# Reading two activations back from DRAM by quarters of columns and turning them on VectorE, in the gate, output-projection and routing stage of a decoder layer

## The chip, the cores and the metric

The kernel runs on one core of a Trainium2 chip, as one launch. The metric is the device time of the whole launch in microseconds (us). Three runs of the kernel before gave 4114.98, 4118.72 and 4122.0 us, so the median is 4118.72 us. PE is TensorE, DVE is VectorE, ACT is ScalarE, POOL is GpSimd and SP is SyncE, whose queue issues most of the DMAs.

## The reference

The layer works on x of 4096 rows and 1024 columns in float32. Two groups of heads, retention (`ret`) and a gated delta rule (`dn`), each make 512 columns. The part that this change touches comes after them:

```python
ret = rmsnorm(ret).reshape(B, T, RET_WIDTH) * jax.nn.silu(r_g.astype(jnp.float32))
...
dn = rmsnorm(dn, dn_norm_w[l]).reshape(B, T, DN_WIDTH) * jax.nn.silu(d_z.astype(jnp.float32))
mix = jnp.concatenate([ret, dn], axis=-1).astype(x.dtype) @ w_out[l]
x = x + gate1[:, None, :] * mix
h2 = modulate(rmsnorm(x, norm2_w[l]), shift2, scale2)
ffn = hierarchical_moe(h2, w_group[l], b_group[l], w_expert[l], b_expert[l], ...)
```

Here `r_g` and `d_z` are columns of the input projection, so their product with `w_in` is also computed in this stage. `hierarchical_moe` first takes the logits of 4 groups and 32 experts (36 columns) of each row of `h2`, picks a group and two experts in it, and later runs the experts on the rows sorted by expert.

## The kernel before

The kernel has four stages. Stage A makes the normed and modulated input, transposed, as a pair of arrays `hh_d` and `hl_d` in DRAM (a rounded part and the remainder), and the retention. Stage B makes the delta rule. Stage C (`phase_c`, `c_tile`, `route`) is the one that changes. Stage D runs the experts.

Precise products are made of three passes of the array: `split` writes a rounded copy of an operand (`hi`, on ScalarE, L71) and the remainder (`lo`, on VectorE, L72), and `proj` (L290 to L292) adds the products `hi`·`hi`, `hi`·`lo` and `lo`·`hi` for each of 8 blocks of 128 input columns. One `proj` with 512 output columns is therefore 24 matmuls.

Stage C goes over 32 tiles of 128 rows. `c_tile` is a generator of one tile's work, cut by `yield` into steps:

1. Load the tile's columns of `hh_d` and `hl_d` and its rows of `ret_d` and `dn_d`. Two `proj` (48 matmuls `pgz`) give the gates, ScalarE applies silu (`sg`), GpSimd multiplies it into `mix`.
2. Turn `mix`: 8 float32 transposes on TensorE into PSUM (`ptm`, L939), then `split` from PSUM into `mh` and `ml`.
3. Two `proj` with `w_out` (48 matmuls `poC`), add to x on VectorE (L946), store x in `acc_d`, square on ScalarE (L950), reciprocal root (`rsqrt_b`, mostly on GpSimd), scale on VectorE (L960), add the shift on GpSimd (L961), store the result in `h2_d`.
4. Turn `h2`: 8 float32 transposes on TensorE (`pth`, L968), copied by ScalarE into `hTC`.
5. The router: 8 float32 matmuls of 36 output rows (`pl`, L979), the bias on VectorE (L980), and at a block's end (4 tiles) a transpose of the logits (`plt`).

`phase_c` calls these steps one tile ahead: the gates of tile t+1 stand before the projection of tile t, and step 5 of tile t-1 after it. `route` then works on a block of tiles, on VectorE for the most part. There are 10 blocks: seven of 4 tiles, one of 2 and two of 1.

The order on each engine is not that of the code. A scheduler works out a list of instructions for each engine, and each engine runs its list strictly in order, waiting at an instruction until its operands are there. The same holds for the DMAs that SP issues. All matmuls of the stage share PE's list, and `acc_d`, `h2_d`, the loads of `hhC`, `hlC`, `mix` and x share SP's.

Of the kernel before, what the change touches and what calls it, by code (L numbers as in the profile page):

```python
# [19 lines left out]
P = 128  # L20
# [33 lines left out]
class Kern:  # L54
# [27 lines left out]
    def wblock(self, src, eng, n=512, extra=None, scale=None, pool=None):  # L82
# [3 lines left out]
        for k2 in range(KD // 2):  # L86
            rows = slice(2 * k2 * P, (2 * k2 + 2) * P)
            raw = two(self.wtile("wraw", F32))
            eng.dma_start(raw[:, :, 0:512], src[rows].rearrange("(a p) n -> p a n", p=P))
# [10 lines left out]
    def setup(self):  # L100
# [8 lines left out]
        self.dn_d = dp.tile([T, 512], F32, name="dn_d")  # L109
        self.h2_d = dp.tile([T, D], F32, name="h2_d")  # L110
# [333 lines left out]
    def phase_b(self):  # L444
        tc, nc, T = self.tc, self.nc, self.T
        with tc.tile_pool(name="B", bufs=2) as p:
# [15 lines left out]
            def next_weights():  # L462
# [5 lines left out]
                self.dnw = self.xp.tile([P, 1], F32, name="dnw", bufs=1)  # L468
                nc.sync.dma_start(self.dnw, self.dn_norm_w.rearrange("o p -> p o"))
# [338 lines left out]
    def phase_c(self):  # L808
        tc, nc, T = self.tc, self.nc, self.T
        with tc.tile_pool(name="C", bufs=2) as p:  # L810
            LG, LT, run = {}, {}, []

            def tile_(t):
                run.append(self.c_tile(p, t, LG, LT))
                next(run[t])
# [6 lines left out]
            self.wo.append(self.wo_block(1, p))  # L822

            self.A2, self.B2 = A2, B2 = [p.tile([P, D], F32, name=n, bufs=1) for n in ("A2", "B2")]
            n2 = p.tile([P, D], F32, name="n2", tag="h2", bufs=2)
# [11 lines left out]
            self.br, self.wr = br, wr  # L837
# [28 lines left out]
            for t in range(NT + 1):  # L866
                if t + 1 < NT:
                    tile_(t + 1)
                if t < NT:
                    next(run[t])  # L870
                if t >= 1:
                    next(run[t - 1])
# [3 lines left out]
                if t < NT:  # L876
                    next(run[t])
# [10 lines left out]
    def wo_block(self, i, pool=None):  # L888
# [5 lines left out]
        def scale(raw, k2):  # L894
            g = g1[:, None].to_broadcast([P, 2, 512])
            if k2 < 2:
                nc.vector.tensor_tensor(raw, raw, g, op=ALU.mult)
            else:
                nc.vector.scalar_tensor_tensor(raw, raw, self.dnw, g, op0=ALU.mult, op1=ALU.mult)

        return self.wblock(self.w_out[0][:, 512 * i:512 * i + 512], nc.scalar, scale=scale, pool=pool)

    def c_tile(self, p, t, LG, LT):
        nc = self.nc
        rows = slice(t * P, (t + 1) * P)
        hs = []
# [680 lines left out]
```

## Time and profile before

| | |
|---|---|
| median of three runs | 4118.72 us |
| the profiled execution's own time | 4121.5 us |
| its span, first to last instruction | 4119.7 us |
| busy over the span: PE, DVE, ACT, POOL | 95%, 60%, 39%, 37% |
| mean DMA rate | 140 GB/s |
| mean granted TensorE clock | 0.981 of full speed |
| stage C, first to last projection | about 1807 to 2625 us |

The profile is one execution of the program. The lines of its views name the line of the code (L939), the engine, the tiles that are written and read, and times. Matmuls overlap in the array, so the time that one occupies PE is read from the distance between starts, or from the chain of waits, which gives each its share. The profiled execution's time is 2.8 us above the median of the runs.

### The profile page before, as it was taken

How to read it: one execution, taken by the hardware profiler on the slowest of the kernel's cores; microseconds unless marked ns; L12 is line 12 of the kernel's file. 1: busy time of each engine (PE TensorE's matmuls, PEld its weight loads, DVE VectorE, ACT ScalarE, POOL GpSimd, SP SyncE). 2: the span in 40 equal slices, each digit the busy share in tenths (PEclk: the TensorE clock that was granted, in tenths of full speed). 3: DMA queues.
4: the chain of work that ended last, by engine and by line, in shares of the span. 5: the costliest groups of instructions: out<-in, count | busy, mean ns of one | idle time of the engine just before them, and what ended most of it. 6: DMA issues, size and time to landing. Idle time of an engine off the chain costs nothing.

```text
span 4119.7 us, 73091 instructions
## 1 busy us (share of the span) xinstructions
PE 3911.6 (95%) x27074; PEld 3515.6 (85%) x27074; DVE 2467.8 (60%) x6437; ACT 1587.3 (39%) x3298; POOL 1525.5 (37%) x2133
## 2 busy tenths in 40 slices
PE   5999999999999999979999999699999999999997
PEld 4888889899999999968888888598888888888886
DVE  6555543577778777742222222557777777777785
ACT  3433443444544444421122211234444444444453
POOL 2333334234443344222333333433333443454442
PEclk9999999999999999989999999799999999999999
DMA  6443322422222222453333333346666675666673
GB/s 194 137 128 123 98 91 89 115 59 74 58 60 66 74 61 60 118 158 120 118 123 123 123 123 111 119 142 209 204 225 226 216 237 193 232 209 206 225 233 125
DMA packets 459759, 577.48 MB, mean 140 GB/s; under 512 B 97296, under 2 KB 361720, under 8 KB 459400
## 3 DMA queue, kind: packets, MB, share of 16 engines
q1 hardware_dynamic: 411112, 464.72, 36.4%
q0 software_dynamic: 45632, 102.64, 7.4%
q10 hardware_dynamic: 2656, 5.42, 0.4%
q8 instruction: 214, 3.51, 0.4%
q14 instruction: 145, 1.19, 0.1%
HBM read 458.94 MB, written 166.78 MB: 152 GB/s over the span
## 4 chain that ended last, share of the span: by engine, by line
PE 77%; DVE 8%; DMA 8%; issue 3%; ACT 2%; SPq 1%; POOL 1%; DVEq 0%; POOLq 0%; ACTq 0%
PE ph L1410 5%; PE ph L1411 5%; PE ph L1409 5%; PE pjB L523 4%; PE pjB L522 4%; PE pjB L524 4%; PE py L1502 3%; PE py L1503 3%; PE py L1504 3%; PE pgz L291 3%; PE pgz L292 3%; PE pgz L290 3%; PE poC L291 3%; PE poC L292 3%; PE poC L290 3%
## 5 line engine op out<-in xcount | busy, mean ns | idle before, releaser
L1410 PE MATMUL ph<-xl,whD 128*128 128x240 f32 (+7 forms) x2048 | 588.2, 288 | 3.5 <-DVE xl L72 3.2
L1409 PE MATMUL ph<-xh,whD 128*128 128x240 f32 (+7 forms) x2048 | 580.1, 289 | 11.6 <-DVE ssD L1330 6.5
L1411 PE MATMUL ph<-xh,wlD 128*128 128x240 f32 (+7 forms) x2048 | 586.4, 288 | 0.0
L71 ACT ACTIVATE whD<-rawD 128x1024 fp32r<-128x1024 f32 x384 | 400.9, 1056 | 316.0 <-PE py L1503 125.9
L72 DVE TENSOR_TENSOR wlD<-rawD,whD 128x1024 fp32r<-128x1024 f32 x384 | 460.9, 1218 | 35.1 <-ACT whD L71 33.2
L522 PE MATMUL pjB<-hhB,whi 128*128 128x260 f32 x1536 | 443.1, 291 | 9.5 <-DVE cv L530 4.2
L523 PE MATMUL pjB<-hlB,whi 128*128 128x260 f32 x1536 | 440.7, 288 | 6.3 <-DMA hlB<-hl_d 6.1
L524 PE MATMUL pjB<-hhB,wlo 128*128 128x260 f32 x1536 | 440.8, 288 | 0.0
L1409 PEld LDWEIGHTS ph<-xh,whD 128*128 128x128 f32 x2048 | 388.9, 191 | 17.6 <-DVE ssD L1330 7.1
L1410 PEld LDWEIGHTS ph<-xl,whD 128*128 128x128 f32 x2048 | 391.1, 191 | 8.2 <-DVE xl L72 5.3
L1411 PEld LDWEIGHTS ph<-xh,wlD 128*128 128x128 f32 x2048 | 390.9, 191 | 1.9
L522 PEld LDWEIGHTS pjB<-hhB,whi 128*128 128x128 f32 x1536 | 289.0, 189 | 13.9 <-DMA hhB<-hh_d 4.5
L523 PEld LDWEIGHTS pjB<-hlB,whi 128*128 128x128 f32 x1536 | 290.3, 189 | 10.7 <-DMA hlB<-hl_d 8.3
L524 PEld LDWEIGHTS pjB<-hhB,wlo 128*128 128x128 f32 x1536 | 290.1, 189 | 1.6
L532 POOL TENSOR_TENSOR cv<-cv,cv 128x256 f32<-128x256 f32 x192 | 142.0, 740 | 399.2 <-DVE Xd L602 140.5
L1502 PE MATMUL py<-whD,hh 128*128 128x512 f32 (+4 forms) x640 | 259.5, 405 | 12.4 <-DVE hh L69 7.6
L1503 PE MATMUL py<-wlD,hh 128*128 128x512 f32 (+4 forms) x640 | 252.8, 395 | 0.0
L1504 PE MATMUL py<-whD,hl 128*128 128x512 f32 (+4 forms) x640 | 245.9, 399 | 4.6 <-DVE hl L72 4.3
L946 DVE TENSOR_TENSOR xC<-poC,xC 128x512 f32<-128x512 f32 x64 | 44.2, 691 | 329.6 <-PE poC L292 329.6
L1537 POOL DMA_INDIRECT acc_d<-ag,to x80 | 112.2, 1403 | 345.9 <-DVE ag L1510 257.9
L530 DVE SCALAR_TENSOR_TENSOR cv<-pjB,cw,cv 128x256 f32<-128x256 f32 x384 | 183.1, 479 | 78.8 <-ACT cv L528 71.5
L290 PE MATMUL pj<-whi,hh 128*128 128x512 f32 x512 | 205.8, 402 | 6.0 <-ACT whi L71 6.0
(449 smaller groups left out, 10234.4 us busy)
## 6 DMA issues: line engine op xcount, KB each, us to landing
rawD<-in_w_dram SPq DMA_DIRECT2D x384, 512.0 KB
wa<-in_w_ada_dram SPq DMA_DIRECT2D x48, 512.0 KB
hhB<-hh_d SPq DMA_DIRECT2D x64, 260.0 KB
hlB<-hl_d SPq DMA_DIRECT2D x64, 260.0 KB
acc_d<-xC SPq DMA_DIRECT2D x32, 520.0 KB
wraw<-in_w_in_dram SPq DMA_DIRECT2D x32, 512.0 KB
hh_d<-hh SPq DMA_DIRECT2D x16, 1024.0 KB
hl_d<-hl SPq DMA_DIRECT2D x16, 1024.0 KB
```

The lines of the kernel that those rows point to most:

```text
L71: nc.scalar.activation(hi, src, AF.Copy)
L72: (e_lo or nc.vector).tensor_tensor(lo, src, hi.bitcast(F32) if hasattr(hi, "bitcast") else hi, op=ALU.subtract)
L290: nc.tensor.matmul(out, a, hi, start=(k == 0), stop=False)
L522: nc.tensor.matmul(pj, wh, hh[k], start=(k == 0), stop=False)
L523: nc.tensor.matmul(pj, wh, hl[k], start=False, stop=False)
L524: nc.tensor.matmul(pj, wl, hh[k], start=False, stop=(k == KD - 1))
L1409: nc.tensor.matmul(ph[nm], hi, xh[:, k, 0:n], start=(k == 0), stop=False)
L1410: nc.tensor.matmul(ph[nm], hi, xl[:, k, 0:n], start=False, stop=False)
L1411: nc.tensor.matmul(ph[nm], lo, xh[:, k, 0:n], start=False, stop=(k == KD - 1))
L1502: nc.tensor.matmul(py[i], a, hi, start=(k == 0), stop=False)
L1503: nc.tensor.matmul(py[i], a, lo, start=False, stop=False)
L1504: nc.tensor.matmul(py[i], b, hi, start=False, stop=(k == 3))
```

## The change

The transposes on TensorE go from the stage, and the router changes its form.

- The gated rows `mix` are stored to a new array `mg_d` in DRAM, and `h2` is stored to `h2_d` as before. A new function `turn` reads the 128 rows back in four DMAs (`seg`), each of 256 columns for 32 partitions, turns 32x32 blocks with two VectorE transposes of 128x512, and splits each half: ScalarE writes the rounded part, VectorE the remainder. This is done for `mix` (into `mh`, `ml`) and for `h2` (into `hT`). To match the new order of the columns, the rows of `w_out` and of the router's weights are loaded in the same order, by more and smaller DMAs.
- The router's product is made of 8 matmuls of the rounded type with 72 output rows and 256 columns in place of the 8 float32 ones, and the four parts are put together by two VectorE operations and one small float32 matmul (`plt`) per tile.
- The gates run two tiles ahead. `rsqrt_b` and the shift of `h2` are on VectorE instead of GpSimd.

```diff
+            if seg:
+                for q in range(4):
+                    r = 256 * q + 64 * k2
+                    eng.dma_start(raw[32 * q:32 * q + 32, :, 0:512], src[r:r + 64].rearrange("(a i) n -> i a n", i=32))
+            else:
+                eng.dma_start(raw[:, :, 0:512], src[rows].rearrange("(a p) n -> p a n", p=P))
...
+        self.mg_d = dp.tile([T, D], F32, name="mg_d")
...
-                self.dnw = self.xp.tile([P, 1], F32, name="dnw", bufs=1)
-                nc.sync.dma_start(self.dnw, self.dn_norm_w.rearrange("o p -> p o"))
+                self.dnw = self.xp.tile([P, KD], F32, name="dnw", bufs=1)
+                nc.vector.memset(self.dnw, 1.0)
+                for q in (2, 3):
+                    for a in range(2):
+                        nc.sync.dma_start(self.dnw[32 * q:32 * q + 32, 4 * a:4 * a + 4],
+                                          self.dn_norm_w.rearrange("o (k i) -> i (o k)", i=32))
...
+        with tc.tile_pool(name="C", bufs=2, reuse_waits="tile") as p:
...
+            tile_(1)
...
-            wr = p.tile([P, KD, 36], F32, name="wr", bufs=1)
-            nc.sync.dma_start(wr[:, :, 0:4], self.w_group[0].rearrange("(k p) n -> p k n", p=P))
-            nc.sync.dma_start(wr[:, :, 4:36], self.w_expert[0].rearrange("(k p) n -> p k n", p=P))
-            br = p.tile([36, 1], F32, name="brt", bufs=1)
+            wr = p.tile([P, KD, 36], F32, name="wr", tag="hT", bufs=1)
+            for q in range(4):
+                w = wr[32 * q:32 * q + 32]
+                for c, src in ((slice(0, 4), self.w_group), (slice(4, 36), self.w_expert)):
+                    nc.sync.dma_start(w[:, :, c], src[0][256 * q:256 * q + 256].rearrange("(k i) n -> i k n", i=32))
+            self.wr = p.tile([P, KD, 72], F32R, name="wr2", bufs=1)
+            self.split(self.wr[:, :, 0:36], self.wr[:, :, 36:72], wr)
...
+            self.sel = p.tile([72, 36], F32, name="sel", bufs=1)
+            nc.vector.tensor_tensor(self.sel, self.ident[0:72, 0:36], self.ident[0:72, 36:72], op=ALU.add)
...
-                if t + 1 < NT:
-                    tile_(t + 1)
+                if t + 2 < NT:
+                    tile_(t + 2)
                 if t < NT:
                     next(run[t])
-                if t >= 1:
-                    next(run[t - 1])
...
                 if t < NT:
+                    next(run[t])
                     next(run[t])
                 if t >= 1:
                     for _ in run[t - 1]:
...
-            g = g1[:, None].to_broadcast([P, 2, 512])
-            if k2 < 2:
-                nc.vector.tensor_tensor(raw, raw, g, op=ALU.mult)
-            else:
-                nc.vector.scalar_tensor_tensor(raw, raw, self.dnw, g, op0=ALU.mult, op1=ALU.mult)
-
-        return self.wblock(self.w_out[0][:, 512 * i:512 * i + 512], nc.scalar, scale=scale, pool=pool)
-
-    def c_tile(self, p, t, LG, LT):
+            for a in range(2):
+                k = 2 * k2 + a
+                nc.vector.scalar_tensor_tensor(raw[:, a], raw[:, a], self.dnw[:, k:k + 1], g1, op0=ALU.mult, op1=ALU.mult)
+
+        return self.wblock(self.w_out[0][:, 512 * i:512 * i + 512], nc.scalar, scale=scale, pool=pool, seg=True)
...
-        mix = []
         for i, d in enumerate((self.ret_d, self.dn_d)):
-            mix.append(self.xp.tile([P, 512], F32, name="mix", tag=f"x{i}", bufs=2))
-            nc.sync.dma_start(mix[i], d[rows, :])
-        for i in range(2):
+            mix = self.xp.tile([P, 512], F32, name="mix", tag=f"x{i}", bufs=2)
+            nc.sync.dma_start(mix, d[rows, :])
             pg = self.psum([P, 512], "pgz", "pj")
             sg = self.xp.tile([P, 512], F32, name="sg", bufs=1)
             self.proj(pg, *hs, 0, self.gz[i], 0, 512)
             nc.scalar.activation(sg, pg, AF.Silu)
-            nc.gpsimd.tensor_tensor(mix[i], mix[i], sg, op=ALU.mult)
+            nc.gpsimd.tensor_tensor(mix, mix, sg, op=ALU.mult)
+            nc.sync.dma_start(self.mg_d[rows, 512 * i:512 * i + 512], mix)
+        yield
+        mh, ml = (p.tile([P, KD, P], F32R, name=n, bufs=1) for n in ("mh", "ml"))
+        self.turn(mh, ml, self.mg_d[rows])
         xw = self.wtile("xC", F32)
         x = xw[:, 0:D]
         nc.gpsimd.memset(xw[:, D:], 0.0)
         nc.sync.dma_start(x, self.x[0, rows, :])
         yield
-
-        if t < 2:
-            mh, ml = ([self.xp.tile([P, 4, P + 2], F32R, name=n, tag="h", bufs=10)[:, :, 0:P] for _ in range(2)]
-                      for n in ("mhx", "mlx"))
-        else:
-            mh, ml = (p.tile([P, KD, P], F32R, name=n, bufs=1).rearrange("p (i k) n -> i p k n", i=2)
-                      for n in ("mh", "ml"))
-        for i in range(2):
-            pt = self.psum([P, 4, P], "ptm", "tp")
-            for a in range(4):
-                nc.tensor.transpose(pt[:, a], mix[i][:, a * P:(a + 1) * P], self.ident)
-            self.split(mh[i], ml[i], pt)
-        yield
         for i in range(2):
             po = self.psum([P, 512], "poC", "ch")
-            self.proj(po, [mh[k // 4][:, k % 4] for k in range(KD)], [ml[k // 4][:, k % 4] for k in range(KD)], 0,
-                      self.wo[i], 0, 512)
+            self.proj(po, [mh[:, k] for k in range(KD)], [ml[:, k] for k in range(KD)], 0, self.wo[i], 0, 512)
             nc.vector.tensor_tensor(x[:, 512 * i:512 * i + 512], po, x[:, 512 * i:512 * i + 512], op=ALU.add)
         nc.sync.dma_start(self.acc_d[rows, :], xw)
         ss = p.tile([P, 1], F32, name="ssC", bufs=2)
-        h2 = p.tile([P, D], F32, name="h2", bufs=2)
+        h2 = self.wtile("h2C", F32)[:, 0:D]
         nc.scalar.activation(h2, x, AF.Square, accum_out=ss)
         nc.vector.tensor_scalar(ss, ss, 1.0 / D, EPS, op0=ALU.mult, op1=ALU.add)
-        last = t == self.NT - 1
-        self.rsqrt_b(p, ss, ss, 1, None if last else nc.gpsimd)
-        if last:
-            for i in range(2):
-                c = slice(512 * i, 512 * i + 512)
-                nc.vector.scalar_tensor_tensor(h2[:, c], x[:, c], ss, self.A2[:, c], op0=ALU.mult, op1=ALU.mult)
-                nc.vector.tensor_tensor(h2[:, c], h2[:, c], self.B2[:, c], op=ALU.add)
-        else:
-            nc.vector.scalar_tensor_tensor(h2, x, ss, self.A2, op0=ALU.mult, op1=ALU.mult)
-            nc.gpsimd.tensor_tensor(h2, h2, self.B2, op=ALU.add)
+        self.rsqrt_b(p, ss, ss, 1)
+        nc.vector.scalar_tensor_tensor(h2, x, ss, self.A2, op0=ALU.mult, op1=ALU.mult)
+        nc.vector.tensor_tensor(h2, h2, self.B2, op=ALU.add)
         nc.sync.dma_start(self.h2_d[rows, :], h2)
         yield
-        hT = self.wtile("hTC", F32)[:, 0:D].rearrange("p (k n) -> p k n", k=KD)
-        for i in range(2):
-            pt = self.psum([P, 4, P], "pth", "tp")
-            for a in range(4):
-                nc.tensor.transpose(pt[:, a], h2[:, (4 * i + a) * P:(4 * i + a + 1) * P], self.ident)
-            nc.scalar.activation(hT[:, 4 * i:4 * i + 4], pt, AF.Copy)
+        hT = p.tile([P, KD, 2, P], F32R, name="hT", bufs=1)
+        self.turn(hT[:, :, 0], hT[:, :, 1], self.h2_d[rows])
         yield
         q, j = self.block_of[t]
         n = len(self.blocks[q])
         if j == 0:
             LG[q] = p.tile([P, 4, 36], F32, name="LG", bufs=1)[:, :n]
-            LT[q] = p.tile([36, 4, P], F32, name="LT", bufs=1)
-        LG, LT = LG[q], LT[q]
-        pl = self.psum([36, P], "pl", "lv")
+
+        pl = self.psum([72, 2, P], "pl", "lv")
         for k in range(KD):
             nc.tensor.matmul(pl, self.wr[:, k], hT[:, k], start=(k == 0), stop=(k == KD - 1))
-        nc.vector.tensor_scalar(LT[:, j], pl, self.br, None, op0=ALU.add)
-        if j == n - 1:
-            pt = self.psum([P, 4, 36], "plt", "tp")
-            for i in range(n):
-                nc.tensor.transpose(pt[:, i], LT[:, i], self.ident[0:36, 0:36])
-            nc.vector.tensor_copy(LG, pt[:, :n])
+        LT = p.tile([72, P], F32, name="LT", bufs=1)
+        nc.vector.tensor_scalar(LT, pl[:, 0], self.br, None, op0=ALU.add)
+        nc.vector.tensor_tensor(LT, pl[:, 1], LT, op=ALU.add)
+        pt = self.psum([P, 36], "plt", "tp")
+        nc.tensor.matmul(pt, LT, self.sel, start=True, stop=True)
+        nc.vector.tensor_copy(LG[q][:, j], pt)
+
+    def turn(self, hi, lo, src):
+
+        nc = self.nc
+        seg = self.wtile("seg", F32)[:, 0:D]
+        for q in range(4):
+            nc.sync.dma_start(seg[32 * q:32 * q + 32].rearrange("j (b c) -> j b c", b=4),
+                              src[:, 256 * q:256 * q + 256].rearrange("(b j) c -> j b c", b=4))
+        for a in range(2):
+            k = slice(4 * a, 4 * a + 4)
+            tr = self.xp.tile([P, 4, P + 2], F32, name="tr", tag="h", bufs=10)[:, :, 0:P]
+            nc.vector.transpose(tr.rearrange("p k (b j) -> p b k j", b=4),
+                                seg.rearrange("p (b k i) -> p b k i", b=4, k=KD)[:, :, k])
+            self.split(hi[:, k], lo[:, k], tr)
```

The `split` at the end of `turn` and the loop of `phase_c` give the list of PE another order at the end of a tile's projection. In these rows `poC` is the projection, `pl` the router and `pgz` the gates. Before, the router's operand `hTC_23636` comes from `h2_23515`, the tile before the one whose projection (`poC_23675`) has just ended:

```order
L290 MATMUL poC_23675<-whi_21054,mh_23620 128x512
L291 MATMUL poC_23675<-wlo_21055,mh_23620 128x512
L292 MATMUL poC_23675<-whi_21054,ml_23621 128x512
L979 MATMUL pl_23727<-hTC_23636,wr_21065 36x128 x8
L984 MATMUL plt_23737<-K_66,LT_23162 128x36 x3
L292 MATMUL pgz_23819<-whi_20673,hlC_23813 128x512
L290 MATMUL pgz_23819<-whi_20673,hhC_23809 128x512
```

With the change `hT_24547` is turned from `h2C_24526`, which is computed from the projection `poC_24498` itself:

```order
L298 MATMUL poC_24498<-wlo_21091,mh_24454 128x512
L299 MATMUL poC_24498<-whi_21090,ml_24455 128x512
L975 MATMUL plt_24573<-sel_21187,LT_24570 128x36
L970 MATMUL pl_24753<-hT_24547,wr2_21180 72x256 x4
L297 MATMUL pgz_24586<-whi_20656,hhC_24576 128x512
L298 MATMUL pgz_24586<-wlo_20657,hhC_24576 128x512
L297 MATMUL pgz_24617<-whi_20723,hhC_24576 128x512
L298 MATMUL pgz_24617<-wlo_20724,hhC_24576 128x512
L970 MATMUL pl_24753<-hT_24547,wr2_21180 72x256 x4
L299 MATMUL pgz_24586<-whi_20656,hlC_24580 128x512
```

So the router's product of a tile has moved from behind the next tile's projection to directly behind its own. Only `plt` stands between the two (at a block's end also the small matmuls of `route`), and the gates of the tile after the next stand behind it.

On SP, before, the store of `h2` is followed by loads that don't depend on it, and nothing in the stage reads `h2_d`:

```order
L917 DMA mix_23557<-ret_d_70 128x512
L917 DMA mix_23559<-dn_d_71 128x512
L962 DMA h2_d_72<-h2_23327 128x1024
L947 DMA acc_d_73<-xC_23241 128x1040
L927 DMA xC_23617<-in_x_dram 128x1024
L911 DMA hlC_24040<-hl_d_69 128x4x128
L911 DMA hlC_24042<-hl_d_69 128x4x128
L911 DMA hhC_24224<-hh_d_68 128x4x128
L911 DMA hhC_24226<-hh_d_68 128x4x128
L917 DMA mix_23815<-ret_d_70 128x512
L917 DMA mix_23817<-dn_d_71 128x512
```

With the change the store is followed at once by the four reads of the same rows, and the loads for the next gates stand behind those:

```order
L950 DMA acc_d_74<-xC_24469 128x1040
L958 DMA h2_d_73<-h2C_24526 128x1024
L983 DMA seg_24548<-h2_d_73 32x4x256 x4
L983 DMA seg_24648<-mg_d_72 32x4x256 x3
L926 DMA hhC_24576<-hh_d_68 128x4x128
L926 DMA hhC_24578<-hh_d_68 128x4x128
L926 DMA hlC_24580<-hl_d_69 128x4x128
L926 DMA hlC_24582<-hl_d_69 128x4x128
L983 DMA seg_24648<-mg_d_72 32x4x256
L944 DMA xC_24661<-in_x_dram 128x1024
L937 DMA mg_d_72<-mix_24584 128x512
L931 DMA mix_25072<-ret_d_70 128x512
```

The loads of `hhC` and `hlC` have thus moved behind a read that waits for the store of `h2`.

On VectorE, before, a tile has two additions, three small operations and the scaling between its projection and the next tile's split:

```order
L946 TENSOR_TENSOR xC_23241<-poC_23461,xC_23241 128x512
L946 TENSOR_TENSOR xC_23241<-poC_23487,xC_23241 128x512
L980 TENSOR_SCALAR LT_23162<-pl_23539,brt_21068 36x128
L951 TENSOR_SCALAR ssC_23514<-ssC_23514 128x1
L431 TENSOR_SCALAR rb_y_23518<-ssC_23514 128x1
L432 TENSOR_SCALAR rb_y_23518<-rb_y_23518 128x1
L960 SCALAR_TENSOR_TENSOR h2_23515<-xC_23241,ssC_23514,A2_21058 128x1024
L72 TENSOR_TENSOR ml_23621<-ptm_23622,mh_23620 128x512
L72 TENSOR_TENSOR ml_23621<-ptm_23629,mh_23620 128x512
L946 TENSOR_TENSOR xC_23429<-poC_23649,xC_23429 128x512
```

With the change (the list from the last round of the reciprocal root on; `seg_24548` is read from `h2_d`, `seg_24648` from `mg_d`):

```order
L442 TENSOR_TENSOR rb_t_24530<-rb_y_24529 128x1
L443 TENSOR_TENSOR rb_t_24530<-rb_t_24530,rb_m_24531 128x1
L445 SCALAR_TENSOR_TENSOR ssC_24525<-rb_t_24530,rb_y_24529 128x1
L956 SCALAR_TENSOR_TENSOR h2C_24526<-xC_24469,ssC_24525,A2_21164 128x1024
L957 TENSOR_TENSOR h2C_24526<-h2C_24526,B2_21165 128x1024
L988 STREAM_TRANSPOSE tr_24553<-seg_24548 128x4x4x32
L988 STREAM_TRANSPOSE tr_24557<-seg_24548 128x4x4x32
L72 TENSOR_TENSOR hT_24547<-tr_24553,hT_24547 128x4x128
L72 TENSOR_TENSOR hT_24547<-tr_24557,hT_24547 128x4x128
L988 STREAM_TRANSPOSE tr_24653<-seg_24648 128x4x4x32
L988 STREAM_TRANSPOSE tr_24657<-seg_24648 128x4x4x32
L972 TENSOR_SCALAR LT_24762<-pl_24753,brt_21183 72x128
```

The last operations of the root, the shift, four transposes and two more remainders have come in, and the transposes of `mix` for the next projection stand behind those of `h2`.

## Rows read from the trace of the kernel before

**Rows 1.** Windows of the stage: stretch, then us; busy us and count by engine; granted clock; DMA share; GB/s.

```profile
1820.00:2625.00 805.00, 800.63 (x3996) 648.69 (x3997) 233.72 (x695) 160.48 (x276) 284.57 (x579) 1.00 0.38 122
```

**Rows 2.** Waits of PE: who waited for whom: total us, times, longest.

```profile
PE poC L290 <- ACT whi L71: 8.1, 2, 7.4
```

**Rows 3.** Chain of waits, 2200 to 2232 us: start, us, what.

```profile
2200.31 0.24 PE pgz L290
...
2216.96 1.87 PE pl L979 x16
2218.83 0.43 PE pgz L292
...
2225.49 0.87 PE ptm L939 x8
2226.36 0.23 PE pgz L290
```

**Rows 4.** Chain of waits in the stage before, 1060 to 1090 us.

```profile
1061.21 0.12 PE pjB L523
...
1067.22 4.92 DMA hlB<-hl_d
1072.15 3.79 DMA dgo<-at
1076.02 0.31 SPq L594
...
1077.30 3.61 DMA L<-dgo
1081.04 0.19 DVE Ltmp L600
```

**Rows 5.** Groups by line and form, whole span, then 1850 to 2600 us: busy, mean ns.

```profile
L72 DVE TENSOR_TENSOR wlD<-rawD,whD 128x1024 fp32r<-128x1024 f32 x384 | 460.9, 1218 | 35.1 <-ACT whD L71 33.2 <-issue 0.3
...
L674 DVE STREAM_TRANSPOSE Tb<-Vb 32x256 f32<-32x256 f32 x32 | 13.8, 432 | 20.0 <-DMA Vb<-dgi 19.6
...
L71 ACT ACTIVATE mh<-ptm 128x512 fp32r<-128x512 f32 x58 | 32.1, 597 | 6.2 <-PE ptm L939 6.2
...
L984 PE MATMUL plt<-K,LT 36*128 36x36 f32 x28 | 4.4, 238 | 0.0
...
L993 DVE TENSOR_TENSOR oh<-el,m 128x32 f32<-128x32 f32 x7 | 1.3, 192 | 0.2
```

**Rows 6.** Timeline 2204 to 2234 us, VectorE, then ScalarE: start, us, engine, line, operation, idle before.

```profile
2217.00 0.69 DVE L946 TENSOR_TENSOR xC<-poC,xC 128x512 f32<-128x512 f32 x1 [4.41 <-PE poC L292]
...
2219.14 0.14 DVE L951 TENSOR_SCALAR ssC<-ssC 128x1 f32<-128x1 f32 x1
2219.31 0.15 DVE L431 TENSOR_SCALAR rb_y<-ssC 128x1 int32<-128x1 int32 x1
...
2224.44 1.28 DVE L960 SCALAR_TENSOR_TENSOR h<-xC,ssC,A 128x1024 f32<-128x1024 f32 x1 [4.79 <-POOL ssC L441]
...
2217.73 1.06 ACT L950 ACTIVATE h<-xC 128x1024 f32<-128x1024 f32 x1 [9.35 <-DVE xC L946]
2218.69 0.19 ACT L950 ACTIVATION_READ_ACCUMULATOR h<-xC 128x1 f32 x1
```

**Rows 7.** DMA issues: what, queue, count, size each.

```profile
dgo<-at SPq DMA_DIRECT2D x64, 32.0 KB
```

**Rows 8.** Windows of 5 us at two restarts of PE.

```profile
1820.00:1825.00 5.00, 5.00 (x16) 3.97 (x17) 2.24 (x2) 0.79 (x1) 0.00 (x0) 0.73 0.96 324
1825.00:1830.00 5.00, 4.80 (x21) 3.57 (x19) 2.51 (x2) 0.63 (x1) 0.00 (x0) 1.00 1.18 286
2675.00:2680.00 5.00, 5.00 (x26) 5.00 (x27) 4.22 (x5) 4.04 (x4) 4.54 (x7) 0.55 0.94 346
```

**Rows 9.** Chain of waits at the stage's end, 2600 to 2682 us.

```profile
2624.78 0.24 PE poC L292
...
2634.29 3.57 PE pl L979 x16
```

More of the change, by code (lines that the diff above doesn't have):

```diff
@@ L80, in wtile, with wblock @@
         return (pool or self.wp).tile([P, 1040], dt, name=name, tag="w", bufs=8 if pool else 27)
-    def wblock(self, src, eng, n=512, extra=None, scale=None, pool=None):
+    def wblock(self, src, eng, n=512, extra=None, scale=None, pool=None, seg=False):
         out = []
@@ L88, in wblock @@
             raw = two(self.wtile("wraw", F32))
-            eng.dma_start(raw[:, :, 0:512], src[rows].rearrange("(a p) n -> p a n", p=P))
+            if seg:
[4 more added lines that the diff above has]
+                eng.dma_start(raw[:, :, 0:512], src[rows].rearrange("(a p) n -> p a n", p=P))
             if extra is not None:
@@ L809, in phase_c @@
         tc, nc, T = self.tc, self.nc, self.T
-        with tc.tile_pool(name="C", bufs=2) as p:
-            LG, LT, run = {}, {}, []
+        with tc.tile_pool(name="C", bufs=2, reuse_waits="tile") as p:
+            LG, run = {}, []
             def tile_(t):
-                run.append(self.c_tile(p, t, LG, LT))
+                run.append(self.c_tile(p, t, LG))
                 next(run[t])
@@ L822, in phase_c @@
             self.wo.append(self.wo_block(1, p))
+            tile_(1)
             self.A2, self.B2 = A2, B2 = [p.tile([P, D], F32, name=n, bufs=1) for n in ("A2", "B2")]
-            n2 = p.tile([P, D], F32, name="n2", tag="h2", bufs=2)
+            n2 = p.tile([P, D], F32, name="n2", tag="hT", bufs=1)
             self.bcast_row(B2, self.mrow_d[:, D:2 * D])
@@ L829, in phase_c @@
             nc.vector.scalar_tensor_tensor(A2, A2, 1.0, n2, op0=ALU.add, op1=ALU.mult)
-            wr = p.tile([P, KD, 36], F32, name="wr", bufs=1)
-            nc.sync.dma_start(wr[:, :, 0:4], self.w_group[0].rearrange("(k p) n -> p k n", p=P))
-            nc.sync.dma_start(wr[:, :, 4:36], self.w_expert[0].rearrange("(k p) n -> p k n", p=P))
-            br = p.tile([36, 1], F32, name="brt", bufs=1)
+            wr = p.tile([P, KD, 36], F32, name="wr", tag="hT", bufs=1)
[5 more added lines that the diff above has]
+            self.split(self.wr[:, :, 0:36], self.wr[:, :, 36:72], wr)
+            self.br = br = p.tile([72, 1], F32, name="brt", bufs=1)
+            nc.vector.memset(br, 0.0)
             nc.sync.dma_start(br[0:4], self.b_group.rearrange("o n -> n o"))
             nc.sync.dma_start(br[4:36], self.b_expert.rearrange("o n -> n o"))
-            self.br, self.wr = br, wr
+            self.sel = p.tile([72, 36], F32, name="sel", bufs=1)
+            nc.vector.tensor_tensor(self.sel, self.ident[0:72, 0:36], self.ident[0:72, 36:72], op=ALU.add)
             ubf = p.tile([P, P], BF, name="ubf", bufs=1)
```

1 line of the change is left out of this document (added).

## The prediction

> **What bounds the kernel now.** I read the busy shares by windows first, then who waits for whom, then the chain of waits in one tile. Over 805 us of the stage PE is busy for 800.63 us at a granted clock of 1.00, while VectorE has 234 us, ScalarE 160 and GpSimd 285 [rows 1]. The longest wait of PE that belongs to the stage is one of 7.4 us, for the split of a `w_out` block at the start [rows 2]. So PE is the bound, and whatever another engine takes is hidden as long as PE's list holds work that is ready.
>
> One tile of the chain runs from the first gate matmul behind the `mix` transposes at 2200.31 us to the next tile's at 2226.36 us: 26.05 us [rows 3]. It holds 96 matmuls of 512 columns, two blocks of 8 transposes at the 0.87 us of the `ptm` row, and the router, 1.87 us and 0.20 us more in the slow start of the matmul behind it (0.43 us where one takes 0.23) [rows 3]. That is 3.81 us for transposes and router. The remaining 22.24 us are 96 matmuls of 0.23 us.
>
> **What PE saves.** All of the 3.81 us go. The new router is 8 matmuls of 256 columns; the nearest row is a matmul of 260 columns of the same type, 0.12 us each in the chain [rows 4], so 0.96 us. The new `plt` is once per tile; a like one lasts 0.24 us [rows 5], taken whole. PE's work falls by 3.81 - 0.96 - 0.24 = 2.6 us, to about 23.45 us per tile. In 32 tiles that is 83 us, if PE still always finds work.
>
> **What PE waits for.** It doesn't find it. In the changed list, directly behind the last matmul of a tile's projection, stand `plt` and then the router of that same tile. Its operand comes out of the whole way from the projection's sum to `h2`, out to DRAM, back, and through the turn. PE works its list in order, so the next gates, which need nothing of this, stand behind it. Before, the router of the tile before stood there, and a full tile of gates and half a projection covered the way. I follow the new way from the end of the last projection matmul. That matmul gives PE free 0.2 us before VectorE can start on its sum at 2217.00 us [rows 6].
>
> - Addition: 0.2 us of that lag and 0.69 us [rows 6]: 0.9 us.
> - Square and its read-out on ScalarE: from 2217.73 us to 2218.69 + 0.19 = 2218.88 us [rows 6]: 1.2 us.
> - The root, now 13 small operations on VectorE (1 for the mean, 3 to start, 3 rounds of 3). Two of them start 0.17 us apart, at 2219.14 and 2219.31 us [rows 6], so with their hand-overs 13 x 0.18 = 2.3 us. Before, GpSimd and its other work put 4.79 us of idle time in front of the scaling [rows 6], which nobody felt.
> - Scaling 1.28 us [rows 6] and shift, like a 1024-column VectorE operation in SBUF, 1.22 us [rows 5]: 2.5 us.
> - Store and four reads. The trace has one such trip through DRAM, in the stage before: store 3.79 us, four loads issued from 1076.02 us, the last one landing 3.61 us after 1077.30 us, and VectorE starting at 1081.04 us [rows 4]. From 1072.15 to 1081.04 us that is 8.9 us, and the store's issue (0.31 us like the load's [rows 4]) makes 9.2; the store is larger now (512 KB against pieces of 32 KB [rows 7]), so 9.3 us.
> - The turn up to the first half's remainder: two transposes of 512 columns, and one remainder. The nearest transpose has 256 columns on 32 partitions and takes 0.43 us [rows 5]; bounds for 512 are 0.43 (as now) and 0.86 (double), and I take 0.70, since it is nearer to double. The rounding on ScalarE, 0.60 us [rows 5], runs beside the second transpose, and the remainder takes half of 1.22 us. Together 2.1 us.
>
> The sum is 0.9 + 1.2 + 2.3 + 2.5 + 9.3 + 2.1 = 18.3 us, of which `plt` covers 0.2: PE stands still for **18.1 us per tile**.
>
> The loads for the next gates stand behind these reads on SP. They are issued while the reads land and the turn runs, so I cost them at nothing; the cover is thin, see the rivals. The gates' own 10 us then cover the read and turn of `mix`, which was stored two tiles earlier. `mix` in DRAM therefore costs little, and the wait is all that of `h2`.
>
> **The clock.** After PE has stood still, rows show it restart at half speed (1.2 GHz) before it is back at 2.4 GHz. After the idle 7.4 us [rows 2] the granted clock is 0.73 in the first 5 us, with PE busy throughout, and 1.00 in the next 5; at a second restart it is 0.55 over 5 us, again with PE busy throughout [rows 8]. The slow part is 2.7 us in one case, and up to 4.5 us in the other, and costs half of itself: 1.35 to 2.25 us per restart, taken as 1.8.
>
> **The sum.** One tile changes by -2.6 + 18.1 + 1.8 = +17.3 us, and this happens behind 31 tiles: +536 us. At a block's end `route` now lies on VectorE between the same addition and the shift: some 22 more operations of about 0.19 us [rows 5] that the square doesn't cover, and a wait for ScalarE's exponentials: 5 us, 9 times, +45 us. The last two tiles have no gates between router and projection, so their `mix` is late by some 3 us each: +6 us. At the end the last tile's tail goes from 12.8 us (last projection matmul at 2624.78 + 0.24 us to the router's end at 2634.29 + 3.57 us [rows 9]) to 18.3 us and a router at half clock of 2 us, +7.5, and its own saving of 2.6 comes off: +5 us. The start, where `w_out` is now loaded in four times as many DMAs, I leave at nothing, within 20 us either way. The total is +592 us on the profiled execution's 4121.5 us: 4713 us, and 2.8 us less against the median, **4710 us**.
>
> **A rule of the Trainium skill.** The trip through DRAM is half of the wait, and its rows are of small pieces: stores of 32 KB [rows 7] that landed after 3.79 us [rows 4]. The Trainium skill's page "DMA: Bandwidth & Descriptors", section "Anatomy of one DMA", gives a fixed 2.0 us per DMA and the bytes over 436 GB/s on the GpSimd path. By that page the store of 512 KB is an estimated 3.2 us and the last read of 128 KB 2.3 us, the trip about 7.1 us, and the sum some 70 us less, 4640 us. The row disagrees with the page at the small size (3.79 against an estimated 2.1 us), and the row goes into my sum.
>
> **Rivals.**
>
> 1. **The wait is longer: the gates' second operand.** The loads of `hlC` are issued on SP behind the reads of `h2`. If SP holds them until the last read has landed, they arrive 0.3 us of issue and 4.92 us (a like load in the chain [rows 4]) after it. PE needs them after the turn (2.1 us) and the router with its first four gate matmuls (1.9 us), so they would be 1.2 us late, and with traffic from the reads of `mix` up to 4 us. Price: 31 x 4 = 124 us, 4830 us. For it: the order on SP. Against: the DMA share of the stage is only 0.38 [rows 1].
> 2. **Faster: the trip is covered.** If PE had at least 18 us of ready work between a tile's projection and its router, as now, only the saving would be left: 4119 - 83 = 4036 us. It decides as soon as the router's place in the list is a gate block further back. PE's busy 800.63 of 805 us [rows 1] shows that such a cover worked; the list of the changed kernel has none of it.
> 3. **The clock does not come back.** If PE with a wait in each tile stayed at half speed, all 23.45 us of a tile would double: another 21.6 x 31 = 670 us, 5380 us. Against it: both restarts end within 5 us [rows 8].
> 4. **The trip is short or the routing hidden.** With 3.61 us for each leg and an issue between them the trip is 7.6 us, and with the blocks' 45 us hidden as well 4710 - 53 - 45 = 4612 us. That is the low part of my forecast.
>
> **How the numbers follow.** A measurement of this kernel tells 0.2% (8 us) from no change. My forecast, with the trip between 7.6 and 11.5 us (two legs of 4.92 us [rows 4] and the issues), the turn at either bound and the restart between 0 and 2.25 us, has a chance of 0.78, and the short trip of rival 4 lies in it. Rival 1 has 0.14, rival 2 has 0.04, rival 3 has 0.03, and 0.01 is left for no change. Low end: trip -53 us, restarts -56 us and routing -40 us, 4560 us. High end: trip +69 us and 100 us of rival 1, 4880 us. Slower has 0.95, faster 0.04, the same 0.01.
>
> **What would show it.** In the profile after, windows of the stage should show PE busy for some 23 to 26 us of each 43 us, the chain of waits should pass in every tile through VectorE's root, the DMA of `h2_d`, the DMA of `seg` and the transposes, and PE's waits should name the split of `hT` at the router, 31 times about 18 us. The granted clock should dip once per tile. I am wrong if PE stays busy through the stage, if the wait sits at the projection for `mh` instead, or if the router's wait is under 10 us.

## The result and the profile after

The changed kernel takes 4613.21 us (median of four runs, 4608.08 to 4617.2), where the kernel before takes 4119.68 us (four runs) beside it. The ratio is 1.1199, with a 95% interval from 1.118 to 1.1218: 12% slower. The profiled execution spans 4612.6 us, 492.9 us more than before.

The rows of the page with the busy times and the granted clock in 40 slices show where:

```profile
PE 3874.6 (84%) x26338; PEld 3489.9 (76%) x26338; DVE 2644.7 (57%) x7034; ACT 1595.7 (35%) x3299; POOL 1375.9 (30%) x1699
...
PEclk9999999999999997777877787777999999999999
```

The clock dips in slices 16 to 28, from 1730 to 3229 us, which hold the stage of the change. Over this stage the windows now read (columns as in [rows 1]):

```profile
1820.00:3118.00 1298.00, 777.16 (x3341) 631.95 (x3341) 408.24 (x1291) 169.54 (x279) 139.19 (x151) 0.78 0.38 110
```

PE is busy 777 of 1298 us, where it was busy 800.63 of 805 [rows 1]. The square of a tile (L953, once per tile) measures the pace by its first and last start; the row is from the list of that line's instructions (after, then before):

```profile
L953 ACT ACTIVATE h2C<-xC x32: 1056/1056/1057, 1838.0 to 3118.7; 128x1024 f32<-128x1024 f32 x32
```

```profile
L950 ACT ACTIVATE h<-xC x32: 1056/1057/1062, 1838.0 to 2625.8; 128x1024 f32<-128x1024 f32 x32
```

The first square starts at the same time in both, and the last one 492.9 us later: the whole loss lies in the 31 steps from tile to tile. The single steps are 26 us before; after they are 41.2 us inside a block and about 44.0 us at a block's end.

PE's longest waits (as [rows 2]):

```profile
PE pl L970 <- DVE hT L72: 388.3, 25, 16.6
PE prk L1074 <- DVE mb L1067: 90.9, 10, 10.0
PE pl L970 <- DVE tr L988: 40.3, 5, 8.3
```

The router waits for the remainder of `hT` 25 times, 15.5 us in the mean. At a block's end the wait is split: first the rank matmuls (`prk`, which count the place of each row among the rows of its expert) wait for `mb`, then the router. One tile in the chain of waits, which answers to [rows 3]:

```profile
2423.40 0.25 PE poC L299
2423.67 0.70 DVE xC L949
2424.39 1.16 ACT h2C L953 x2
2427.96 1.29 DVE h2C L956
2429.28 1.24 DVE h2C L957
2430.53 2.61 DMA h_d<-h2C
2433.16 0.32 SPq L983
...
2434.47 3.04 DMA seg<-h_d
2437.71 0.72 DVE tr L988
2438.45 0.64 ACT hT L71
2439.12 0.70 DVE hT L72
2439.95 1.10 PE pl L970 x4
2441.05 0.43 PE pgz L297
```

From the end of the projection (2423.65) to the router (2439.95) 16.3 us pass, and nothing of PE stands in between. The first gates behind the router then take 0.43 us each, where one takes 0.23 [rows 3].

### The profile page after: what moved, and what is told of

Read it like the earlier page. It is cut to its first block, busy times and chain, and to the rows that moved or that the text cites. A ratio compares the mean times of both kernels' runs of the same rounds, so it can differ in the third digit from the quotient of the medians.

```text
span 4612.6 us, 72336 instructions
## 1 busy us (share of the span) xinstructions
PE 3874.6 (84%) x26338; PEld 3489.9 (76%) x26338; DVE 2644.7 (57%) x7034; ACT 1595.7 (35%) x3299; POOL 1375.9 (30%) x1699
## 4 chain that ended last, share of the span: by engine, by line
PE 67%; DVE 12%; DMA 11%; issue 4%; ACT 3%; SPq 2%; POOL 0%; DVEq 0%; ACTq 0%; POOLq 0%
PE ph L1415 5%; PE ph L1416 4%; PE ph L1414 4%; PE pjB L533 3%; PE pjB L534 3%; PE pjB L535 3%; PE pgz L297 3%; PE poC L297 3%; PE pgz L298 3%; PE poC L298 3%; PE poC L299 3%; PE py L1507 3%; PE py L1508 3%; PE py L1509 3%; PE pgz L299 2%
## 5 line engine op out<-in xcount | busy, mean ns | idle before, releaser
L970 PE MATMUL pl<-hT,wr 128*72 128x256 f32 x256 | 65.3, 403 | 445.1 <-DVE hT L72 388.3
L970 PEld LDWEIGHTS pl<-hT,wr 128*72 128x72 f32 x256 | 51.2, 227 | 457.0 <-issue 429.0
L949 DVE TENSOR_TENSOR xC<-poC,xC 128x512 f32<-128x512 f32 x64 | 44.3, 691 | 530.6 <-PE poC L299 530.6
L988 DVE STREAM_TRANSPOSE tr<-seg 128x512 f32<-128x512 f32 x128 | 83.6, 691 | 304.1 <-DMA seg<-h_d 195.5
```

## Experiments

All ratios are against the kernel before, run beside each on the same chip.

**h2 turned on PE again.** The router's weights are loaded in plain row order, and in `c_tile` (in all code cuts, `...` stands for lines left out):

```diff
-        self.turn(hT[:, :, 0], hT[:, :, 1], self.h2_d[rows])
...
+            for a in range(4):
+                nc.tensor.transpose(pt[:, a], h2[:, (4 * i + a) * P:(4 * i + a + 1) * P], self.ident)
+            self.split(hT[:, k, 0], hT[:, k, 1], pt)
```

> The changed kernel with the normed row h2 turned by eight TensorE transposes again (the store to DRAM stays, for the experts); mix still goes through DRAM and VectorE. In its list PE finds a router of the tile before behind each projection, and gates behind it. Theory A (the loss is the h2 trip that PE meets with nothing ready behind it): the 16 us of waiting per tile go. A tile is 26.05 us less 0.87 for the mix transposes, less 0.9 for the router, plus 0.24 for plt, some 24.5 us: 4119 - 32 x 1.5 = 4070 us (4040 to 4130 with what the block ends cost). Theory B (the mix half, or SP's longer list of DMAs with it, costs the time): the loss stays for the most part, over 4450 us.

Measured: 4091.3 us, ratio 0.9924 [0.9907, 0.994]. The loss is gone, and a little gained. The windows show PE busy throughout:

```profile
1840.00:2540.00 700.00, 700.00 (x3353) 574.63 (x3352) 345.39 (x1068) 153.46 (x256) 130.17 (x136) 1.00 0.57 171
```

So the mix half through DRAM costs nothing in the steady part. But this run changes two things, since the scheduler also wrote another list: the router now stands behind the next tile's projection.

**mix turned on PE again.** The product of `mix` goes into a tile in SBUF, `w_out` is loaded in plain row order, and:

```diff
-        self.turn(mh, ml, self.mg_d[rows])
...
+            for a in range(4):
+                nc.tensor.transpose(pt[:, a], mx[:, (4 * i + a) * P:(4 * i + a + 1) * P], self.ident)
+            self.split(mh[:, k], ml[:, k], pt)
```

> The changed kernel with mix turned by eight TensorE transposes again and never stored to DRAM (w_out and its weights in their plain row order); h2 still goes out to DRAM and comes back to VectorE. PE's list keeps the router of a tile behind that tile's own projection, with four gate matmuls in between. Theory A (the h2 trip is the loss): the wait stays, the transposes add 0.87 x 32 = 28 us, the shorter SP list takes up to 1 us per tile off: 4610 us (4570 to 4660). Theory B (the mix half is the loss): under 4200 us.

Measured: 4258.18 us, ratio 1.0325 [1.0306, 1.0345], between both theories. I had misread the list of this kernel: here too the scheduler put the router of tile T-1 behind the projection of tile T. The wait sits elsewhere, in PE's waits and in SP's timeline:

```profile
PE pgz L297 <- DMA hhC<-hh_d: 100.6, 29, 5.4
```

```profile
2301.95 0.32 SPq L961 DMA_DIRECT2D h_d<-h2C  x1
2304.69 1.75 SPq L986 DMA_DIRECT2D seg<-h_d  x4
2306.53 0.93 SPq L924 DMA_DIRECT2D hhC<-hh_d  x2
2307.51 1.05 SPq L924 DMA_DIRECT2D hlC<-hl_d  x2
```

The first read of `h2` is issued when the store has landed, 2.7 us after its issue. The loads of the next gates stand behind the four reads, and PE waits for them, 3.5 us in the mean. This is close to my first rival, in a kernel where the router no longer covers it. But SP holds the loads only until the reads are issued (2306.44 us), not until they have landed, and PE waits for `hhC`, not for `hlC`.

**A longer way.** Root and shift back on GpSimd, with PE's list unchanged:

```diff
-        self.rsqrt_b(p, ss, ss, 1)
+        self.rsqrt_b(p, ss, ss, 1, nc.gpsimd)
...
-        nc.vector.tensor_tensor(h2, h2, self.B2, op=ALU.add)
+        nc.gpsimd.tensor_tensor(h2, h2, self.B2, op=ALU.add)
```

> The changed kernel with the root and the shift of h2 on GpSimd, as before; PE's list is unchanged. The way from the projection to the store of h2 gets longer: the root 13 operations some 0.275 us apart and two hand-overs instead of 2.3 us on VectorE (+1.5 to +2.0 us), the shift 2.40 us instead of 1.22 and a hand-over (+1.2 to +1.4). Theory A (every microsecond of the h2 way is a microsecond of the tile): +3.0 us x 31 = +93 us, 4706 us (4690 to 4725). Theory B (another wait runs beside the h2 way and ends last, the gates' loads for one): less than +30 us.

Measured: 4717.17 us, ratio 1.145 [1.1427, 1.1473], 104 us above the changed kernel, 3.4 us per tile. In its chain the addition in front starts at 2421.09 us and the router at 2440.02 us, so the way is longer by 2.7 us; the rest of the 3.4 us lies behind the router. The way of `h2` is the time of the tile, and what runs beside it doesn't catch it when it gets longer. Theory A holds.

**The place of the router alone.** PE's groups of matmuls (gates, projection, router) are tied, the first matmul of each behind the last of the group before, in the order of the program (`router(T-1)` behind `proj(T)`):

```diff
+    def behind(self, first, last):
+        if self.link is not None:
+            self.tc.add_manual_dep(first.ins, self.link.ins.name, ...)
+        self.link = last
```

> The changed kernel with one thing more: PE's order of gates, projections and routers is tied together, so that the router of tile T-1 stands behind the projection of tile T, and gates behind it. The loads stay as they are: the turned pieces of h2 share the ring of the gates' operands, so on SP the next gates' loads stand behind the read of h2. Theory A (the router's place is the loss, and what comes next is the gates' loads behind the read): the 16 us go, and a wait for hhC of 5 to 8 us per tile takes their place, as in the run with mix on PE (5 us, 30.5 us per tile). About 30.5 to 32 us per tile instead of 41.3: 4613 - 31 x 10 = 4300 us (4230 to 4360). Theory B (the place is enough): 4036 to 4120 us. Theory C (the place decides nothing, the DMA traffic does): over 4500 us.

Measured: 4658.23 us, ratio 1.1306 [1.1275, 1.1336]. Theory A missed, and so did B: the place alone gains nothing, and costs 1% more than the change. By its number it would be C, but not by its reason: the DMA share is 0.38 over 1900 to 2500 us, and the fastest kernel below has 0.67. PE's waits and SP's order tell it:

```profile
PE pgz L306 <- DMA hhC<-hh_d: 378.3, 29, 16.6
```

```profile
2402.74 0.32 SPq L970 DMA_DIRECT2D h_d<-h2C  x1
2405.40 1.74 SPq L997 DMA_DIRECT2D seg<-h_d  x4
2407.24 1.32 SPq L997 DMA_DIRECT2D seg<-mg_d  x3
2408.61 0.98 SPq L938 DMA_DIRECT2D hhC<-hh_d  x2
2409.69 1.00 SPq L938 DMA_DIRECT2D hlC<-hl_d  x2
```

The 16 us moved from the router to the gates: 378.3 us in 29 waits, 13 us each. Their loads are issued 5.9 to 8 us behind the `h2` store, in this kernel as in the changed one.

**The loads alone.** The order of PE is kept as in the changed kernel (`router(T)` behind `proj(T)`), and the turned pieces leave the ring that the gates' operands use:

```diff
-            tr = self.xp.tile([P, 4, P + 2], F32, name="tr", tag="h", bufs=10)[:, :, 0:P]
+            tr = self.psum([P, 4, P], "tr", "tp")
```

> The other half of the pair: PE's order is tied as in the changed kernel (projection of T, router of T, gates, projection of T+1), and only the loads are freed: the turned pieces lie in PSUM, so that the next gates' loads are issued ahead of the read of h2. Theory A (two waits in parallel, the router's for h2 on PE and the gates' loads behind the h2 read on SP, each long enough by itself): nothing gained, the wait stays at the router with 16 us per tile, 4590 us (4560 to 4640; the rank matmuls stand inside a projection here, up to 22 us). Theory B (the loads alone were the cause): under 4300 us.

Measured: 4624.33 us, ratio 1.1212 [1.1193, 1.123], no different from the change. PE's waits name the router again:

```profile
PE pl L981 <- DVE hT L72: 520.5, 32, 16.6
```

**Both.** The tied order of the run on the place, and the pieces in PSUM.

> The kernel of the tied order, and the turned pieces now lie in PSUM, so that the gates' loads no longer stand behind the read of h2 on SP; the read of mix still does. Theory A (each thing that SP holds behind the h2 read becomes the next wait): the wait for hhC is gone, and one for mh at the projection of some 6 to 9 us per tile is there: issued behind the h2 read some 14 us after a projection's end, landed 18 us after it, turned 20.5 us after it, and wanted 12.3 us after it. 4119 - 83 + 31 x 8 = 4284 us (4220 to 4340). Theory B (only the gates' loads were left): 4036 to 4130 us.

Measured: 4396.1 us, ratio 1.0669 [1.0638, 1.0699]. Only both together take something off, 217 of the 493 us. The time is above the range of theory A, and the rest isn't where I expected most of it. PE's longest waits of the stage:

```profile
PE plt L989 <- DVE hT L72: 224.2, 31, 15.3
PE poC L306 <- ACT mh L71: 79.1, 32, 24.3
```

Three rows of its timelines, VectorE and then PE, show why most of it sits at `plt`:

```profile
2328.65 0.29 DVE L987 TENSOR_TENSOR LT<-pl,LT 72x128 f32<-72x128 f32 x1
...
2345.04 1.29 DVE L72 TENSOR_TENSOR hT<-tr,hT 128x512 fp32r<-128x512 f32 x2
...
2345.78 0.64 PE L989 MATMUL plt<-sel,LT 72*128 72x36 f32 x2 [6.41 <-DVE hT L72]
```

The operand `LT` is ready at 2328.94 us. `plt` starts at 2345.78 us, just when the first of the two remainders of 0.7 us has read `tr`: it takes its PSUM buffer from the ring of two where `tr` now lies. So the way of `h2` still holds PE, through a third path, a shared ring of buffers. The run that takes `plt` out of this ring, below, tests that in a kernel close to this one.

**Router back, loads free, mix read ahead.** The read of `mix` of the next tile also moves in front of the projection:

```diff
+                if t + 1 < NT:
+                    next(run[t + 1])
                 if t < NT:
                     next(run[t])
...
```

> Both rows still go through DRAM and are turned on VectorE, but the order is written out: PE takes gates, projection and router of the tile before in turn (router of tile T-1 behind the projection of tile T), the turned pieces lie in PSUM instead of the ring that the gates' loads share, and mix of the next tile is read before the projection. The h2 way then has a router, 48 gate and 48 projection matmuls in front of its router, 23 us against the 16.3 us that it takes. Theory A: only the saving on PE is left, 4119 - 2.6 x 32 = 4036 us (4020 to 4090 with the block ends). Theory B (DMA traffic or SP's list is too slow for two trips per tile, wherever the router stands): over 4300 us.

Measured: 4092.47 us, ratio 0.9924 [0.9908, 0.9941]. Both trips through DRAM are there in each tile, and the kernel is faster than before. The time lies 2.5 us above the range of theory A, and 56 us above its 4036 us. PE waits 36 us in 15 waits at `plt`, most of it for the remainder of `hT`:

```profile
PE plt L998 <- DVE hT L72: 30.0, 13, 8.3
```

**Router two places back.** The router of T-1 also behind the gates of the next but one.

> The kernel of the run that put the router one tile back (4092 us), with the router now behind the next gates as well: projection of T, gates of T+3, router of T-1, projection of T+1, so that h2 has 11 us more of cover. In the run before, PE waited 36 us in 15 waits for hT and 15 us for the ranks of a block. Theory A (what is left above 4036 are these waits, since h2's way got longer with the second turn on VectorE and the traffic): some 30 to 45 us come off, 4055 us (4040 to 4070). Theory B (what is left is the start of the stage and its last two tiles): no change, 4085 to 4100 us.

Measured: 4091.06 us, ratio 0.9925 [0.9902, 0.9947]. No change: 11 us of further cover for the router don't touch the wait of `plt`, so theory A fell with its cause, and the time is in the range of theory B.

**The bias on ScalarE**, in the kernel with the router one tile back:

```diff
-        nc.vector.tensor_scalar(LT, pl[:, 0], self.br, None, op0=ALU.add)
-        nc.vector.tensor_tensor(LT, pl[:, 1], LT, op=ALU.add)
+        nc.scalar.activation(LT, pl, AF.Identity, bias=self.br)
```

> The kernel with the router one tile back (4092 us), with the two bias additions behind the router taken off VectorE: PE sums both parts in PSUM (16 matmuls of 128 columns instead of 8 of 256), and one ScalarE operation adds the bias. In that kernel, PE waited 36 us at plt, because the additions stand behind the turn of h2 in VectorE's list. Theory A (VectorE's list is the third queue behind the h2 read): these waits go, 30 to 45 us, 4055 us (4040 to 4070). Theory B (what is left is at the start of the stage and in its last tiles): 4080 to 4100 us.

Measured: 4083.24 us, ratio 0.991 [0.9894, 0.9927]. The medians are 9 us apart and the intervals overlap. The cause assumed here, VectorE's list, was wrong: in the kernel with the router one tile back an `LT` is ready at 2284.35 us, and its `plt` starts at 2305.25 us, just behind the first remainder of `hT` (from 2304.42 us). PE's list changed along with this edit: `plt` now stands inside a projection.

**plt in a buffer of its own.**

```diff
-        pt = self.psum([P, 36], "plt", "tp")
+        pt = self.psum([P, 36], "plt", "lv")
```

> The kernel with the router one tile back (4092 us), with one thing moved: plt gets its PSUM buffer from the ring of pl instead of the ring of two that it shares with the turned pieces. In the trace of that kernel plt starts 0.1 us after the first remainder of hT, though its operand LT was ready 20 us before: it waits for a buffer, not for VectorE's list (which the run with ScalarE's addition had assumed). Theory A (the shared PSUM ring holds PE, and these waits are time): the 36 us of waits at plt go, and 20 to 36 us come off: 4065 us (4056 to 4075). Theory B (another wait takes their place): 4080 to 4100 us.

Measured: 4061.33 us, ratio 0.9849 [0.9832, 0.9867]: 1.5% faster than the kernel before, the best of all. The windows and PE's longest wait of the stage:

```profile
1840.00:2540.00 700.00, 694.35 (x3222) 566.61 (x3222) 401.42 (x1200) 154.67 (x266) 133.38 (x145) 1.00 0.67 195
```

```profile
PE poC L306 <- ACT mh L71: 24.0, 1, 24.0
```

A step is now 23.5 us in most tiles. The longest waits left in the stage are this one, of the first projection for its `mix`, which now makes the trip too, and 14.9 us of the rank matmuls in the last tiles. They aren't lost whole: the first square starts 1.2 us later than before (1839.2 us), the third one 7 us later (1884.8 us). Which of them makes the 25 us that are left above 4036 us was not tried.

**The clock: filling the wait.** Behind each projection of the changed kernel come matmuls whose result nobody reads:

```diff
+        for j in range(60):
...
+            f = nc.tensor.matmul(fill, w[:, 0:P], w[:, 0:512], start=True, stop=True)
...
```

> The changed kernel with 60 more matmuls of 512 columns behind every projection (some 13.9 us at 0.23 us, into a PSUM tile that nobody reads), so that PE works through most of the wait for h2; the h2 way and the place of the router are the same, and the rank matmuls of a block's end come behind the gates instead of ahead of the router. Theory A (the restart at half clock costs 1.35 to 2.25 us per tile): the first gates behind the router take 0.23 us each instead of 0.43, and 31 x 1.6 = 50 us come off, with up to 22 us more at the block ends (2.8 us each, 8 times): 4563 us (4530 to 4590). Theory B (the clock costs nothing that the wait doesn't hide): 4600 to 4625 us.

Measured: 4592.17 us, ratio 1.1159 [1.1124, 1.1194], which overlaps the changed kernel's; the median is between both theories. The fill ended too early: PE still stood still for 2.6 us in front of the router (66.1 us in 25 waits), and in 24 of 29 tiles the first gates took 0.43 us as before. Two windows of 5 us around one such restart, with the granted clock in the third column from the right:

```profile
2420.00:2425.00 5.00, 2.32 (x12) 1.89 (x11) 2.39 (x5) 1.22 (x2) 0.00 (x0) 0.97 1.14 237
2425.00:2430.00 5.00, 5.00 (x20) 4.20 (x20) 1.85 (x5) 0.76 (x2) 0.00 (x0) 0.69 0.89 241
```

With 72 matmuls:

> The kernel with filling matmuls behind every projection, now 72 of them instead of 60 (72 x 0.231 = 16.6 us, against the 16.0 us after which the router's operand is ready), so that PE never stands still there. With 60 it still stood still for 2.6 us in front of the router, and the first four gates took 0.43 us each all the same. Theory A (the restart at half clock costs 1.35 to 2.25 us per tile): the router's and the first gates' matmuls run at 0.06 and 0.23 us, which takes 1.6 us off a tile, and the fill's overhang puts 0.6 us on: some 30 us below the run with 60, 4560 us (4535 to 4580). Theory B (the half clock costs nothing that isn't hidden): 4592 us or, with the overhang, up to 4615 us.

Measured: 4563.85 us, ratio 1.1076 [1.1057, 1.1094], 49 us below the changed kernel. The granted clock of the stage:

```profile
1840.00:3000.00 1160.00, 1147.99 (x5188) 935.48 (x5187) 385.58 (x1159) 157.62 (x258) 126.37 (x136) 1.00 0.41 117
```

Theory A holds: more work for PE made the kernel faster, since its clock stayed at 2.4 GHz. The rank matmuls moved as well, so the 49 us aren't the clock's price alone. With 60 they had moved in the same way, and from 60 to 72 the time falls by 28 us. PE's starts give the price in a tile: from the router's first matmul to the first of the next projection it is 13.6 us in the changed kernel and 12.5 us here (medians), 1.1 us.

## Why the prediction was right, and where it was off

The sign, the place and the mechanism came as forecast: the time is within the range, near its low end, and the short trip of rival 4 is what happened. That its number (4612 us) is met within 1 us is luck, as the terms below show.

- **The way of h2.** By the steps of the prediction the chain reads 0.7, 1.2, 2.4, 2.6, 7.2 and 2.2 us, together 16.3, where 0.9, 1.2, 2.3, 2.5, 9.3 and 2.1 were forecast. Five of six terms hold within 0.2 us; what is missing in the first is the lag of 0.2 us, which is 0.02 here (2423.65 to 2423.67 us). The mis-sized term is the **trip through DRAM**: 2430.53 to 2437.71 us, 7.2 us instead of 9.3, 65 us in 31 tiles. The row that I took [rows 4] is from another stage, of pieces of 32 KB [rows 7]. Why the smaller store took longer there isn't shown.
- **The rule on the trip.** Of the measured 7.2 us the store took 2.61 us, the issues of the reads 1.3 us and the last read 3.04 us. By the Trainium skill's page "DMA: Bandwidth & Descriptors", section "Anatomy of one DMA", whose fit is for DMAs that GpSimd issues (these are issued by SP), the trip is an estimated 7.1 us, with 3.2 us for the store and 2.3 us for the read. The trace agrees with that sum, but not with its parts, whose errors cancel.
- **Block ends.** A step at a block's end takes 2.8 us more than the others; before the change it was already 0.9 us more (27.0 against 26.1 us). So seven of them cost some 13 us, not 45. Most of `route`'s operations still stand ahead of the store of `h2`, but they run between those of the root. From the addition to the store it is 9.4 us there (2505.85 to 2515.21 us) instead of 6.9 us.
- **The sum by stretches.** For the first two steps I forecast 34.6 us more than before, for the 27 steps behind them with all block ends 512.1 us, and for the last two and the tail 45.6 us, together 592 us. By the starts of the squares it was 44.3, 420.7 and 27.8 us, together 493, and nothing is lost behind the last square. Of the 91 us in the middle, the trip makes 57 and the block ends 32. Rival 4 has -53 us for the trip and -45 for the blocks, so its sum is met by errors that cancel.
- **The saving of PE** was invisible in the changed kernel and exact: the 23.45 us per tile are the steps of 23.5 us of the best run.
- **The clock.** The half clock at the restart is in the chain (four gates at 0.43 us), and the fill of 72 showed that it costs time. The cost was mis-sized: 1.1 us per tile by PE's starts, where I took 1.8 from rows that gave 1.35 to 2.25.
- **The step that failed.** In rival 2 I wrote of the cover: "It decides as soon as the router's place in the list is a gate block further back." The run that moved only the router gave 4658 us. There were **two waits side by side**: the router for `h2` on PE, and the gates' loads behind the `h2` read on SP. I costed the second at nothing, which is right for the sum, since it ran beside the first. As the cause of the loss it is just as much one: either alone keeps all of it (4658 and 4624 us). Without both 217 us of 493 go (4396 us), since `plt` and `tr` then share a ring in PSUM; with the read of `mix` moved ahead as well, which also changed the place of `plt` in PE's list, all of it goes (4092 us). The reason on SP isn't the change's idea but a ring of buffers that `tr` shares with the gates' operands.

One reading of the list before was off, though no sum uses it: the cover was not "a full tile of gates and half a projection" but 48 gate and 8 of the 48 projection matmuls up to the transposes of `h2`, and the whole projection up to the router.

What I named as tests came mostly so: the chain passes through root, store, read and transposes, and the granted clock dips. The wait at the router is 15.5 us, 25 times, not 18 us 31 times.

## What to carry to other kernels

When a step of a chain is sent through DRAM, look at every list in which its parts now stand: the consumer's engine, the queue that issues the read, and the rings of buffers that its new tiles share. A wait removed in one of them gives nothing while another of the same length runs beside it, so undo them one at a time and then together before naming the cause. A list that a scheduler writes is part of the edit: print it for every variant.

## What the runs showed that I had not expected

- PE at 2.4 GHz went on at full speed behind some stops and not behind others of the same length. In the run with 60 filling matmuls, stops of 2.4 to 3.7 us were followed by gates of 0.43 us in 24 tiles, and stops of 2.4 to 3.1 us by gates of 0.23 us in 5. In the run with `mix` on PE, 13 of 21 stops of 3.0 to 3.4 us were followed by full speed and 8 by gates of 0.43 us. One of the 13 is from 2306.8 to 2309.95 us; the windows there read

```profile
2305.00:2310.00 5.00, 1.85 (x9) 1.17 (x7) 0.89 (x2) 0.15 (x1) 0.00 (x0) 1.00 0.87 213
2310.00:2315.00 5.00, 4.79 (x24) 3.73 (x25) 2.76 (x6) 1.08 (x2) 0.00 (x0) 1.00 0.75 206
```

  So the length of the stop alone doesn't tell; what does stays open.
- A store of 512 KB landed in 2.61 us and a read of 128 KB behind it in 3.04 us, both less than the 3.79 us of the store of small pieces in the stage before, and the 3.61 us of the load behind it [rows 4].
